# The block steps of the delta net's triangular inverse, eight heads at a time and on two quarters of the array

## The chip, the core and the metric

The kernel runs on one core of one Trainium2 chip. The metric is the time of one execution on the device in microseconds; the time of the kernel before is the median of 3 runs.

## What is computed

A block of two decoder layers and a third mixed layer on 256 tokens of width 1024, all in float32. The change lies in the first layer, a gated delta net with 16 value heads of width 128. The reference works in chunks of 64 tokens and solves a unit lower triangular system for each head and chunk:

```python
m = jnp.where(strict, jnp.einsum('bnhcd,bnhsd->bnhcs', k_beta, k) * decay, 0.0)
t_mat = lax.linalg.triangular_solve(m + eye, eye, left_side=True, lower=True, unit_diagonal=True)
u = jnp.einsum('bnhcs,bnhse->bnhce', t_mat, v_beta)
w = jnp.einsum('bnhcs,bnhsd->bnhcd', t_mat, k_beta * jnp.exp(gc)[..., None])
...
v_new = u_i - jnp.einsum('bhcd,bhde->bhce', w_i, state)
o_i = jnp.einsum('bhcd,bhde->bhce', qd_i, state) + jnp.einsum('bhcs,bhse->bhce', a_i, v_new)
```

The output of each head is normalized, gated with silu(z) and multiplied by `w_out`; convolution-gated feed-forward layers and two kinds of attention follow.

## The kernel before

The kernel computes the same with two blocks of 128 tokens (`tt` = 0, 1) per head instead of four chunks of 64. `XA` holds for each head three 128x128 blocks: the two diagonal ones (index 0 and 2) and the one across (index 1); `EA` holds the same of the decayed query-key products. The inverse of a diagonal block is made in levels. `inv_stage` inverts all 32x32 diagonal blocks by substitution on VectorE, with tokens of four blocks on the partitions, and DMAs write them back into `XA` and, transposed, into `T64`, which lies in the memory of `h`. Then come two doublings, 32 to 64 and 64 to 128: with inverses A and B of two neighbouring blocks and the block C between them, the new corner is a product of three, made in two steps. `y1` (line 823) and `z1` (lines 833, 834) are these steps for 32x32 blocks, `y2` (847) and `z2` (855) for 64x64. Each matmul of `y1` uses a 32x32 tile of the array, and `j` = 0, 2 are two tiles in different row and column groups; `z1` has a third. `y2` reads partitions 0 to 63 and writes 64 to 127 (the quarter of the rows `lo` and columns `hi`); `z2` reads 64 to 127 and writes 0 to 63. Between the steps ScalarE and VectorE copy the results out of PSUM (lines 824, 825, 835 to 838, 848, 857).

`chain(q4)` does this for four heads and then their recurrence: `y0p` (867), `x10p` (873), `y1p` (879), the outputs `o0p` and `o1p` (890 to 894), squares on ScalarE (898), a small chain of [128, 8] operations for the reciprocal root (905 to 910, with `rsqrt` at 334 to 338), eight scalings with silu(z) (913), and the transposes `otp` (921), whose copies `oh`, `ol` are the operands of the output product. `z` was parked in DRAM (`wzd`, line 803), and comes back by POOL's DMA as `wzog` (886) into a buffer that `kT` and `qT` hold before.

The order of the work: `gemm` and `gemm_nat` run the weight products in program order, and after every four weight tiles `w` calls `tick`, which advances each generator in `self.sides` by one `yield`. So the chains' pieces are strewn between the products of `w_in` (`pb`; 512 columns wide for z). `CY` = 2 and `CZ` = 2 ticks lie between a chain's steps. A chain starts when the chain before it has done its levels:

```python
def chain(q4):
    while not (st["inv"] and st["v"] >= 2 * q4 + 2 and st["lev"] >= q4):
        yield
```

Before `y0p` it also waits until `og` of the chain two before is counted. The products with `w_out` (`acc`) start when three of chain 0's heads are there. A list scheduler then sets each engine's order by its own estimate. Each weight block of 128x1024 is split by ScalarE into `wh` (line 186) and by VectorE into `wl` (187), and each product is three matmuls (249 to 251). PSUM has 8 banks; `acc` holds four. PE, ScalarE, VectorE and POOL each work in order.

Of the kernel before, what the change touches and what calls it, by code (L numbers as in the profile page):

```python
# [13 lines left out]
AF = mybir.ActivationFunctionType  # L14
# [5 lines left out]
P = 128  # L20
# [98 lines left out]
CY = 2  # L119
# [23 lines left out]
class Builder:  # L143
# [432 lines left out]
    def gdn_body(self, gp, x):  # L576
        nc, tc, sp = self.nc, self.tc, self.sp
        big = lambda nm: gp.tile([P, 8, T], F32, tag="big", bufs=2, name=nm)
        t4 = lambda sh, nm, dt=F32: gp.tile(sh, dt, tag="t4", bufs=2, name=nm)
        t2 = lambda sh, nm, dt=F32: gp.tile(sh, dt, tag="t2", bufs=6, name=nm)  # L580
        blk = lambda b: slice(32 * b, 32 * b + 32)
# [140 lines left out]
        def a_stage():  # L722
            while st["X"] < 8 or st["qss"] < 4 or st["step"] < AWAIT:
                yield
            factors(16)
            nc.vector.tensor_scalar(rq, rk.rearrange("p (a c) -> p a c", c=8)[:, 2:4], P ** -0.5, None, ALU.mult)
            for j in range(8):
                kq = self.bank("kq")
                nc.tensor.matmul(kq[:, 0:T], kT[:, j, 0:P], qT[:, j], start=True, stop=True)
                nc.tensor.matmul(kq[:, T:384], kT[:, j, P:], qT[:, j, P:], start=True, stop=True)  # L730
                for h in (2 * j, 2 * j + 1):
                    nc.vector.scalar_tensor_tensor(EA[:, h, 0:2], ev2(kq[:, 0:T]), negc[:, h : h + 1], EA[:, h, 0:2], ALU.mult, ALU.mult)
                    nc.vector.scalar_tensor_tensor(EA[:, h, 2], kq[:, T:384], negc[:, 16 + h : 17 + h], EA[:, h, 2], ALU.mult, ALU.mult)
                st["A"] = j + 1
                for _ in range(ASTEP):
                    yield
# [5 lines left out]
        T64 = self.h.rearrange("p a t -> p (a t)").rearrange("p (a h c) -> p a h c", a=2, h=16)  # L742
# [65 lines left out]
        hs = lambda i: slice(i * P, i * P + P)  # L808
        oks = {}

        def chain(q4):
            while not (st["inv"] and st["v"] >= 2 * q4 + 2 and st["lev"] >= q4):
                yield
            H = slice(4 * q4, 4 * q4 + 4)
            heads = range(4 * q4, 4 * q4 + 4)
            cs = slice(512 * q4, 512 * q4 + 512)
            Y1 = t2([P, 2, 4, 32], "Y1")
            b = self.bank("y1p")
            bv = b[:, 0:256].rearrange("p (a h c) -> p a h c", a=2, h=4)
            for tt in range(2):  # L820
                for i, h in enumerate(heads):
                    for j in (0, 2):
                        nc.tensor.matmul(bv[blk(j + 1), tt, i], XA[blk(j), h, 2 * tt, blk(j + 1)], T64[blk(j), tt, h, 0:32], start=True, stop=True)
            nc.scalar.activation(Y1[blk(1)], bv[blk(1)], AF.Copy)
            nc.vector.tensor_copy(Y1[blk(3)], bv[blk(3)])
            for _ in range(CY):
                yield
            b = self.bank("z1p")
            bv = b.rearrange("p (k a h c) -> p k a h c", k=2, a=2, h=4)
            for tt in range(2):  # L830
                for i, h in enumerate(heads):
                    for j in (0, 2):
                        nc.tensor.matmul(bv[blk(j), 0, tt, i], Y1[blk(j + 1), tt, i], XA[blk(j + 1), h, 2 * tt, blk(j + 1)], start=True, stop=True)
                    nc.tensor.matmul(bv[blk(1), 1, tt, i], XA[blk(1), h, 2 * tt, blk(1)], Y1[blk(1), tt, i], start=True, stop=True)
            nc.scalar.activation(T64[blk(1), :, H, 0:32], bv[blk(1), 1], AF.Copy)
            for tt in range(2):
                nc.vector.tensor_copy(XA[blk(0), H, 2 * tt, blk(1)], bv[blk(0), 0, tt])
                nc.scalar.activation(XA[blk(2), H, 2 * tt, blk(3)], bv[blk(2), 0, tt], AF.Copy)
            for _ in range(CY):
                yield  # L840
            lo, hi = slice(0, 64), slice(64, 128)
            Y2 = t2([P, 2, 4, 64], "Y2")
            b = self.bank("y2p")
            bv = b.rearrange("p (a h c) -> p a h c", a=2, h=4)
            for tt in range(2):
                for i, h in enumerate(heads):
                    nc.tensor.matmul(bv[hi, tt, i], XA[lo, h, 2 * tt, hi], T64[lo, tt, h], start=True, stop=True)  # L847
            nc.scalar.activation(Y2[hi], bv[hi], AF.Copy)
            for _ in range(CY):
                yield  # L850
            b = self.bank("z2p")
            bv = b.rearrange("p (a h c) -> p a h c", a=2, h=4)
            for tt in range(2):
                for i, h in enumerate(heads):
                    nc.tensor.matmul(bv[lo, tt, i], Y2[hi, tt, i], XA[hi, h, 2 * tt, hi], start=True, stop=True)  # L855
# [9 lines left out]
            b = self.bank("y0p")  # L865
# [5 lines left out]
            b = self.bank("x10p")  # L871
# [5 lines left out]
            b = self.bank("y1p")  # L877
# [1058 lines left out]
```

## Time and profile before

| | |
|---|---|
| median of 3 runs | 1217.02 us (1215.78 to 1218.51) |
| the profiled execution | 1216.23 us |
| its span | 1214.4 us |
| granted TensorE clock | 0.997 |
| PE, PEld busy | 98%, 93% of the span |
| DVE, ACT, POOL busy | 74%, 57%, 2% |

The span is the time from the first to the last instruction in the profile. PE is TensorE's matmuls, PEld its weight loads, DVE is VectorE, ACT is ScalarE, POOL is GpSimd. A line of a timeline gives the start, the length of the group from its first start to its last end, the operation with output <- inputs, and, in brackets, how long the engine had been idle and what released it. Matmuls are pipelined: their lengths overlap, and the distance between starts is what one takes of PE's time. In the names, `a<-b,c` leaves out buffer numbers; `xh`, `xl` are the split input.

### The profile page before, as it was taken

What the parts mean: (1) busy time and instruction counts of PE and PEld (TensorE: products, weight loads), DVE (VectorE), ACT (ScalarE), POOL (GpSimd) and SP (SyncE); (2) the same over time, 40 slices, a digit from 0 to 9 for tenths busy, and PEclk for the clock granted to TensorE, in tenths of its full rate; (3) what the DMA queues carried; (4) which work ended last, traced back from release to release, by engine and by line L of the source; (5) the groups of instructions that cost most, each with busy time, mean ns of one, the idle gap of its engine ahead of it and who ended that gap; (6) DMA issues with size and microseconds to landing.
All of it is one profiled execution on the core that took longest, in us unless ns stands there. A gap on an engine that the chain in (4) does not pass through costs nothing.

```text
span 1214.4 us, 23416 instructions
## 1 busy us (share of the span) xinstructions
PE 1188.7 (98%) x9368; PEld 1125.4 (93%) x9368; DVE 895.2 (74%) x1680; ACT 687.7 (57%) x1170; POOL 20.4 (2%) x47
## 2 busy tenths in 40 slices
PE   7999989999999999999999999999999999999997
PEld 6989878999999999889999999889789999999996
DVE  6978976668877778878977778756756567655555
ACT  5785547546655556656755556754465445444443
POOL 1000000000000000000000000000000000000000
PEclk9999999999999999999999999999999999999999
DMA  6546365355555557435555564364255563555552
GB/s 222 179 132 216 125 192 183 124 157 168 199 184 182 187 179 243 126 115 161 190 188 183 187 191 158 112 207 134 87 161 173 188 234 118 186 179 187 189 179 83
DMA packets 68318, 206.01 MB, mean 170 GB/s; under 512 B 18198, under 2 KB 18342, under 8 KB 67953
## 3 DMA queue, kind: packets, MB, share of 16 engines
q1 hardware_dynamic: 65600, 194.77, 50.3%
q0 software_dynamic: 2608, 9.75, 2.2%
q8 instruction: 73, 1.20, 0.4%
q14 instruction: 37, 0.29, 0.1%
HBM read 199.75 MB, written 4.74 MB: 168 GB/s over the span
## 4 chain that ended last, share of the span: by engine, by line
PE 92%; DVE 4%; ACT 2%; DMA 1%; issue 1%; SPq 0%; DVEq 0%; ACTq 0%
PE pb L249 21%; PE pb L250 20%; PE pb L251 20%; PE acc L249 7%; PE acc L250 7%; PE acc L251 7%; DVE wl L187 1%; PE pt L1138 1%; PE ssb L669 1%; DMA wr<-wall 0%; DMA h<-xT 0%; PE z2p L855 0%; PE y2p L847 0%; PE kv L1542 0%; PE csum L366 0%
## 5 line engine op out<-in xcount | busy, mean ns | idle before, releaser
L187 DVE TENSOR_TENSOR wl<-wr,wh 128x1024 fp32r<-128x1024 f32 x362 | 441.5, 1223 | 193.7 <-ACT wh L186 192.3
L186 ACT ACTIVATE wh<-wr 128x1024 fp32r<-128x1024 f32 x362 | 381.6, 1057 | 338.3 <-issue 101.1
L251 PE MATMUL pb<-xh,wl 128*128 128x256 f32 x1224 | 345.6, 283 | 3.9 <-DVE wl L187 3.9
L249 PE MATMUL pb<-xh,wh 128*128 128x256 f32 x1224 | 347.8, 284 | 0.6 <-ACT xh L569 0.6
L250 PE MATMUL pb<-xl,wh 128*128 128x256 f32 x1224 | 345.5, 282 | 0.2 <-DVE xl L570 0.2
L249 PEld LDWEIGHTS pb<-xh,wh 128*128 128x128 f32 x1224 | 231.7, 189 | 2.8 <-issue 1.3
L251 PEld LDWEIGHTS pb<-xh,wl 128*128 128x128 f32 x1224 | 229.7, 188 | 4.5 <-DVE wl L187 4.5
L250 PEld LDWEIGHTS pb<-xl,wh 128*128 128x128 f32 x1224 | 230.1, 188 | 0.5 <-DVE xl L570 0.4
L249 PE MATMUL pb<-fh,wh 128*128 128x256 f32 x416 | 118.3, 285 | 0.0
L250 PE MATMUL pb<-fl,wh 128*128 128x256 f32 x416 | 117.5, 283 | 0.1
L251 PE MATMUL pb<-fh,wl 128*128 128x256 f32 x416 | 116.6, 281 | 0.0
L249 PE MATMUL acc<-ah,wh 128*128 128x256 f32 x352 | 98.7, 280 | 0.0
L251 PE MATMUL acc<-ah,wl 128*128 128x256 f32 x352 | 98.5, 280 | 0.0
L250 PE MATMUL acc<-al,wh 128*128 128x256 f32 x352 | 98.5, 280 | 0.0
L249 PEld LDWEIGHTS pb<-fh,wh 128*128 128x128 f32 x416 | 77.9, 188 | 1.4 <-issue 0.4
L250 PEld LDWEIGHTS pb<-fl,wh 128*128 128x128 f32 x416 | 78.1, 188 | 1.1 <-DVE fl L436 0.3
L251 PEld LDWEIGHTS pb<-fh,wl 128*128 128x128 f32 x416 | 78.9, 190 | 0.0
L977 DVE SCALAR_TENSOR_TENSOR fy<-fpad,cols,fy 128x256 f32<-128x256 f32 x176 | 73.6, 478 | 0.0
L249 PE MATMUL pb<-wh,xh 128*128 128x512 f32 (+1 forms) x176 | 70.5, 402 | 0.0
L250 PE MATMUL pb<-wl,xh 128*128 128x512 f32 (+1 forms) x176 | 68.1, 387 | 0.5 <-DVE wl L187 0.5
L251 PE MATMUL pb<-wh,xl 128*128 128x512 f32 (+1 forms) x176 | 68.0, 387 | 0.0
L249 PEld LDWEIGHTS acc<-ah,wh 128*128 128x128 f32 x352 | 66.9, 190 | 0.0
(437 smaller groups left out, 2091.2 us busy)
## 6 DMA issues: line engine op xcount, KB each, us to landing
wr<-wall SPq DMA_DIRECT2D x362, 512.0 KB, 3.6
wzd<-zt POOLq DMA_DIRECT2D x8, 256.0 KB, 3.0
wzog<-wzd POOLq DMA_DIRECT2D x4, 512.0 KB, 5.2
bias<-bd POOLq DMA_DIRECT2D x4, 512.0 KB, 7.7
h<-xT SPq DMA_DIRECT2D x4, 256.0 KB, 4.0
h<-xT POOLq DMA_DIRECT2D x1, 1024.0 KB, 5.9
wrow<-wrow POOLq DMA_DIRECT2D x1, 1024.0 KB, 10.0
out_dram<-mw SPq DMA_DIRECT2D x4, 256.0 KB, 2.0
```

Of the source, the lines that this page charges most:

```text
L186: nc.scalar.activation(hi, r, AF.Copy)
L187: i = nc.vector.tensor_tensor(lo, r, hi.bitcast(F32), ALU.subtract)
L249: mm(out, ah, bh, start=start, stop=False, skip_group_check=skip)
L250: mm(out, ah, bl, start=False, stop=False, skip_group_check=skip)
L251: mm(out, al, bh, start=False, stop=stop, skip_group_check=skip)
L669: nc.tensor.matmul(ssb[:, c : c + 1], sq[:, i, tt * P : tt * P + P], self.ones[:, 0:1], start=True, stop=True)
L977: nc.vector.scalar_tensor_tensor(y[:, i], u[:, i, j : j + T], w(j), y[:, i], ALU.mult, ALU.add)
L1138: nc.tensor.transpose(pt[:, j * P : j * P + P], S[:, i, j * P : j * P + P], self.ident)
```

## The change

The levels leave `chain` and become one generator `levels` for all heads, with two batches of eight heads (`g` = 0, 1). A step's copies are 512 columns wide, `z1` has two banks (its third tile writes `z1q`), and `y2` and `z2` have a bank for each `tt`. The second batch is a step behind the first, and `yz2(1, 0)` issues `y2` of batch 1 and `z2` of batch 0 matmul by matmul in turns. `chain(q4)` starts when its batch has been counted in `lev`, so chains 0 and 1 start together, and chains 2 and 3.

```diff
+        def y1(g):
+            Y1[g] = t2([P, 2, 8, 32], "Y1")
+            b = self.bank("y1p")
+            for tt in range(2):
+                for i, h in enumerate(hds(g)):
+                    for j in (0, 2):
+                        nc.tensor.matmul(b4(b)[blk(j + 1), tt, i], XA[blk(j), h, 2 * tt, blk(j + 1)], T64[blk(j), tt, h, 0:32], start=True, stop=True)
+            nc.scalar.activation(Y1[g][blk(1)], b4(b)[blk(1)], AF.Copy)
+            nc.vector.tensor_copy(Y1[g][blk(3)], b4(b)[blk(3)])
+
+        def z1(g):
+            b0, b1 = self.bank("z1p"), self.bank("z1q")
+            for tt in range(2):
+                for i, h in enumerate(hds(g)):
+                    for j in (0, 2):
+                        nc.tensor.matmul(b4(b0)[blk(j), tt, i], Y1[g][blk(j + 1), tt, i], XA[blk(j + 1), h, 2 * tt, blk(j + 1)], start=True, stop=True)
+                    nc.tensor.matmul(b4(b1)[blk(1), tt, i], XA[blk(1), h, 2 * tt, blk(1)], Y1[g][blk(1), tt, i], start=True, stop=True)
...
+        def yz2(gy, gz):
...
+            for tt in range(2):
+                for i in range(8):
+                    if gy is not None:
+                        h = 8 * gy + i
+                        nc.tensor.matmul(b3(by[tt])[hi, i], XA[lo, h, 2 * tt, hi], T64[lo, tt, h], start=True, stop=True)
+                    if gz is not None:
+                        h = 8 * gz + i
+                        nc.tensor.matmul(b3(bz[tt])[lo, i], Y2[gz][hi, tt, i], XA[hi, h, 2 * tt, hi], start=True, stop=True)
...
+                st["lev"] += 2
+
+        def levels():
+            while not st["inv"]:
+                yield
+            steps = [lambda: y1(0), lambda: (z1(0), y1(1)), lambda: (yz2(0, None), z1(1)), lambda: yz2(1, 0), lambda: yz2(None, 1)]
+            for f in steps:
+                f()
+                for _ in range(CY):
+                    yield
+
         def chain(q4):
-            while not (st["inv"] and st["v"] >= 2 * q4 + 2 and st["lev"] >= q4):
+            while st["lev"] <= q4 or st["v"] < 2 * q4 + 2:
                 yield
...
-            for tt in range(2):
-                for i, h in enumerate(heads):
-                    nc.tensor.matmul(bv[hi, tt, i], XA[lo, h, 2 * tt, hi], T64[lo, tt, h], start=True, stop=True)
-            nc.scalar.activation(Y2[hi], bv[hi], AF.Copy)
-            for _ in range(CY):
-                yield
...
-            for tt in range(2):
-                nc.vector.tensor_copy(XA[lo, H, 2 * tt, hi], bv[lo, tt])
-            st["lev"] += 1
...
+        self.side(levels())
         for q4 in range(4):
             self.side(chain(q4))
```

How the instructions of the engines move shows in their order. First PE in the block steps, before. The listing names an fp32 matmul once; the trace shows two records of it. The `pb` rows are products of `w_in`.

```order
L823 MATMUL y1p<-h,XA 32x32 x15
L833 MATMUL z1p<-XA,Y_1976 32x32
...
L833 MATMUL z1p<-XA,Y_1976 32x32
L834 MATMUL z1p<-Y_1976,XA 32x32
L833 MATMUL z1p<-XA,Y_1976 32x32 x2
L834 MATMUL z1p<-Y_1976,XA 32x32
...
L847 MATMUL y2p<-h,XA 64x64 x8
...
L855 MATMUL z2p<-XA,Y_2105 64x64 x8
L823 MATMUL y1p<-h,XA 32x32 x16
```

And after:

```order
L825 MATMUL y1p<-h,XA 32x32 x31
L834 MATMUL z1p<-XA,Y_1976 32x32
L835 MATMUL z1q<-Y_1976,XA 32x32 x16
L825 MATMUL y1p<-h,XA 32x32 x19
L834 MATMUL z1p<-XA,Y_1976 32x32 x16
L825 MATMUL y1p<-h,XA 32x32 x13
...
L834 MATMUL z1p<-XA,Y_1976 32x32 x15
...
L849 MATMUL y2p<-h,XA 64x64 x8
L849 MATMUL y2q<-h,XA 64x64 x8
L834 MATMUL z1p<-XA,Y_2104 32x32 x2
L835 MATMUL z1q<-Y_2104,XA 32x32
...
L849 MATMUL y2p<-h,XA 64x64
L852 MATMUL z2p<-XA,Y_2200 64x64
```

The steps of four heads stood apart, between products; now those of eight heads stand together, the first `z1` with its third tile (`z1q`) on its own, the later one with three tiles in turn, and the middle pass with `y2` and `z2` in turn.

Second, VectorE at the same place, where `wl` is what the next products of `w_in` read and `EA` needs the product `kq` on PE. Before:

```order
L732 SCALAR_TENSOR_TENSOR EA<-kq,fac,EA 128x256
L733 SCALAR_TENSOR_TENSOR EA<-kq,fac,EA 128x128
L187 TENSOR_TENSOR wl_2002<-wr_1917,wh_2001 128x1024
L732 SCALAR_TENSOR_TENSOR EA<-kq,fac,EA 128x256
L187 TENSOR_TENSOR wl_2081<-wr_1949,wh_2080 128x1024
```

And after:

```order
L187 TENSOR_TENSOR wl_2018<-wr_1917,wh_2017 128x1024
...
L187 TENSOR_TENSOR wl_2158<-wr_1949,wh_2157 128x1024
...
L187 TENSOR_TENSOR wl_2264<-wr_2015,wh_2263 128x1024
L732 SCALAR_TENSOR_TENSOR EA<-kq,fac,EA 128x256
L733 SCALAR_TENSOR_TENSOR EA<-kq,fac,EA 128x128
```

The `wl` that stood behind a pair of `EA` operations now stand, three of them, ahead of it.

Third, the place where the products of `w_in` end and those of `w_out` begin. PE before:

```order
L249 MATMUL pb<-wh_2265,xh 128x512
L250 MATMUL pb<-wl_2266,xh 128x512
L251 MATMUL pb<-wh_2265,xl 128x512
L873 MATMUL x10p<-yy,XA 128x128 x4
L847 MATMUL y2p<-h,XA 64x64 x8
L921 MATMUL otp<-ident,wzog 128x128 x8
L879 MATMUL y1p<-r_2433,XA 128x128 x4
L890 MATMUL o0p<-yy,EA 128x128 x4
L855 MATMUL z2p<-XA,Y_2490 64x64 x8
L823 MATMUL y1p<-h,XA 32x32 x16
L249 MATMUL acc<-oh,wh_2307 128x256
```

PE after:

```order
L249 MATMUL pb<-wh_2427,xh 128x512
L250 MATMUL pb<-wl_2428,xh 128x512
L251 MATMUL pb<-wh_2427,xl 128x512
L937 MATMUL otp<-ident,wzog 128x128 x5
L883 MATMUL y0p<-vn,XA 128x128 x6
L937 MATMUL otp<-ident,wzog 128x128 x3
L883 MATMUL y0p<-vn,XA 128x128 x2
L937 MATMUL otp<-ident,wzog 128x128 x8
L249 MATMUL acc<-oh,wh_2516 128x256
...
L889 MATMUL x10p<-yy,XA 128x128 x8
```

and VectorE after, from the second chain's small operations on (`rq_2527` and `rq_2554` are the factors of chains 0 and 1):

```order
L921 TENSOR_TENSOR sc<-ms,rq_2554 128x8
L336 TENSOR_TENSOR rst<-rsy 128x8
L922 TENSOR_TENSOR sc<-sc,rq_2554 128x8
...
L926 SCALAR_TENSOR_TENSOR sc<-rsy,rq_2527 128x8
L336 TENSOR_TENSOR rst<-rsy 128x8
L929 SCALAR_TENSOR_TENSOR wzog<-o0p,sc,wzog 128x128 x4
L929 SCALAR_TENSOR_TENSOR wzog<-o1p,sc,wzog 128x128 x4
L337 SCALAR_TENSOR_TENSOR rst<-rst,sc 128x8
L187 TENSOR_TENSOR wl_2678<-wr_2514,wh_2677 128x1024
...
L926 SCALAR_TENSOR_TENSOR sc<-rsy,rq_2554 128x8
L929 SCALAR_TENSOR_TENSOR wzog<-o0p,sc,wzog 128x128 x4
L929 SCALAR_TENSOR_TENSOR wzog<-o1p,sc,wzog 128x128 x4
```

Before, the transposes of one chain stand there, with other steps of the next ones behind them; now those of two chains, with `y0p` of the next pair between, and ahead of all `acc`. VectorE does the small operations of two chains in turns, and a `wl` stands between their scalings.

## Rows read from the trace of the kernel before

**Rows 1.** The page: span, and busy time of PE and its weight loads.

```profile
span 1214.4 us, 23416 instructions
PE 1188.7 (98%) x9368; PEld 1125.4 (93%) x9368; DVE 895.2 (74%) x1680; ACT 687.7 (57%) x1170; POOL 20.4 (2%) x47
```

**Rows 2.** Busy time by stretch: start:end, length, PE, PEld, DVE, ACT, POOL, clock, DMA share, GB/s.

```profile
163.00:183.00 20.00, 17.81 (x241) 16.18 (x241) 13.57 (x29) 7.88 (x14) 0.00 (x0) 1.00 0.58 189
...
206.50:277.00 70.50, 70.34 (x698) 68.73 (x697) 45.91 (x116) 38.70 (x95) 2.70 (x5) 1.00 0.44 145
```

**Rows 3.** Timeline of PE, 163 to 200 us: start, length, count, [idle <- releaser].

```profile
169.75 0.24 PE L833 MATMUL z1p<-XA,Y 32*32 32x32 f32 x2 [0.46 <-ACT Y L824]
...
173.67 0.28 PE L249 MATMUL pb<-xh,wh 128*128 128x256 f32 x1
173.88 1.14 PE L847 MATMUL y2p<-h,XA 64*64 64x64 f32 x16
...
175.17 0.28 PE L251 MATMUL pb<-xh,wl 128*128 128x256 f32 x1
...
178.07 0.39 PE L251 MATMUL pb<-xh,wl 128*128 128x256 f32 x1 [1.72 <-DVE wl L187]
...
180.33 0.28 PE L251 MATMUL pb<-xh,wl 128*128 128x256 f32 x1
...
181.62 0.69 PE L823 MATMUL y1p<-h,XA 32*32 32x32 f32 x32
...
182.46 0.28 PE L250 MATMUL pb<-xl,wh 128*128 128x256 f32 x1
...
184.11 1.05 PE L867 MATMUL y0p<-vn,XA 128*128 128x128 f32 x8
185.09 0.22 PE L833 MATMUL z1p<-XA,Y 32*32 32x32 f32 x2
...
185.60 0.19 PE L834 MATMUL z1p<-Y,XA 32*32 32x32 f32 x1
...
186.06 0.40 PE L250 MATMUL pb<-wl,xh 128*128 128x512 f32 x1
...
186.99 0.40 PE L251 MATMUL pb<-wh,xl 128*128 128x512 f32 x1
```

**Rows 4.** Durations in ns, min/median/max, of the steps' matmuls and copies (views by tile).

```profile
L847 PE MATMUL y2p<-h,XA x64: 218/218/267, 173.9 to 223.7; 64*64 64x64 f32 x64
...
L824 ACT ACTIVATE Y<-y1p x4: 374/375/376, 169.3 to 213.1; 32x256 f32<-32x256 f32 x4
...
L848 ACT ACTIVATE Y<-y2p x4: 575/592/597, 177.3 to 225.6; 64x512 f32<-64x512 f32 x4
```

**Rows 5.** The z copies: POOL's timeline, issue to landing (page), and the silu behind them.

```profile
190.17 1.07 POOL L886 DMA_DIRECT2D wzog<-wzd  x2 [27.78 <-PE kq L730]
...
wzog<-wzd POOLq DMA_DIRECT2D x4, 512.0 KB, 5.2
...
L887 ACT ACTIVATE wzog<-wzog x4: 1048/1057/1059, 195.2 to 233.1; 128x1024 f32<-128x1024 f32 x4
```

**Rows 6.** Timelines of PE, ScalarE and VectorE at the end of chain 3.

```profile
248.31 0.37 PE L249 MATMUL acc<-oh,wh 128*128 128x256 f32 x1
...
254.05 0.33 PE L921 MATMUL otp<-ident,wzog 128*128 128x128 f32 x1
...
248.59 0.28 ACT L898 ACTIVATE wzog<-o1p 128x128 f32<-128x128 f32 x1 [0.54 <-PE o1p L894]
...
249.77 0.17 DVE L905 TENSOR_TENSOR sc<-ms,rq 128x8 f32<-128x8 f32 x1 [0.46 <-ACT wzog L898]
...
253.64 1.13 DVE L913 SCALAR_TENSOR_TENSOR wzog<-o0p,sc,wzog 128x128 f32<-128x128 f32 x4
```

**Rows 7.** The page's costliest groups: VectorE's `wl`, busy us and mean ns.

```profile
L187 DVE TENSOR_TENSOR wl<-wr,wh 128x1024 fp32r<-128x1024 f32 x362 | 441.5, 1223 | 193.7 <-ACT wh L186 192.3
```

**Rows 8.** Waits of PE's weight loads, 163 to 277 us: total, times, longest.

```profile
PEld otp L921 <- DVE wzog L913: 0.5, 2, 0.3
```

More of the change, by code (lines that the diff above doesn't have):

```diff
@@ L809, in gdn_body @@
         oks = {}
+        lo, hi = slice(0, 64), slice(64, 128)
+        Y1, Y2 = {}, {}
+        hds = lambda g: range(8 * g, 8 * g + 8)
+        h8 = lambda g: slice(8 * g, 8 * g + 8)
+        b4 = lambda b: b.rearrange("p (a h c) -> p a h c", a=2, h=8)
+        b3 = lambda b: b.rearrange("p (h c) -> p h c", h=8)
+        def y1(g):
[7 more added lines that the diff above has]
+            nc.vector.tensor_copy(Y1[g][blk(3)], b4(b)[blk(3)])
@@ new lines, in z1 @@
+        def z1(g):
[5 more added lines that the diff above has]
+                    nc.tensor.matmul(b4(b1)[blk(1), tt, i], XA[blk(1), h, 2 * tt, blk(1)], Y1[g][blk(1), tt, i], start=True, stop=True)
+            H = h8(g)
+            nc.scalar.activation(T64[blk(1), :, H, 0:32], b4(b1)[blk(1)], AF.Copy)
+            for tt in range(2):
+                nc.vector.tensor_copy(XA[blk(0), H, 2 * tt, blk(1)], b4(b0)[blk(0), tt])
+                nc.scalar.activation(XA[blk(2), H, 2 * tt, blk(3)], b4(b0)[blk(2), tt], AF.Copy)
@@ new lines, in yz2 @@
+        def yz2(gy, gz):
+            by = [self.bank("y2p"), self.bank("y2q")] if gy is not None else None
+            bz = [self.bank("z2p"), self.bank("z2q")] if gz is not None else None
+            for tt in range(2):
+                for i in range(8):
[5 more added lines that the diff above has]
+                        nc.tensor.matmul(b3(bz[tt])[lo, i], Y2[gz][hi, tt, i], XA[hi, h, 2 * tt, hi], start=True, stop=True)
+            if gy is not None:
+                Y2[gy] = t4([P, 2, 8, 64], "Y2")
+                for tt in range(2):
+                    nc.scalar.activation(Y2[gy][hi, tt], b3(by[tt])[hi], AF.Copy)
+            if gz is not None:
+                for tt in range(2):
+                    nc.vector.tensor_copy(XA[lo, h8(gz), 2 * tt, hi], b3(bz[tt])[lo])
+                st["lev"] += 2
@@ L816, in chain @@
             cs = slice(512 * q4, 512 * q4 + 512)
-            Y1 = t2([P, 2, 4, 32], "Y1")
-            b = self.bank("y1p")
-            bv = b[:, 0:256].rearrange("p (a h c) -> p a h c", a=2, h=4)
-            for tt in range(2):
-                for i, h in enumerate(heads):
-                    for j in (0, 2):
-                        nc.tensor.matmul(bv[blk(j + 1), tt, i], XA[blk(j), h, 2 * tt, blk(j + 1)], T64[blk(j), tt, h, 0:32], start=True, stop=True)
-            nc.scalar.activation(Y1[blk(1)], bv[blk(1)], AF.Copy)
@@ L825, in chain @@
-            nc.vector.tensor_copy(Y1[blk(3)], bv[blk(3)])
-            for _ in range(CY):
-                yield
-            b = self.bank("z1p")
-            bv = b.rearrange("p (k a h c) -> p k a h c", k=2, a=2, h=4)
-            for tt in range(2):
[L831 to L844, printed above, removed]
@@ L845, in chain @@
-            for tt in range(2):
-                for i, h in enumerate(heads):
-                    nc.tensor.matmul(bv[hi, tt, i], XA[lo, h, 2 * tt, hi], T64[lo, tt, h], start=True, stop=True)
-            nc.scalar.activation(Y2[hi], bv[hi], AF.Copy)
[L849 to L855, printed above, removed]
@@ L856, in chain @@
-            for tt in range(2):
-                nc.vector.tensor_copy(XA[lo, H, 2 * tt, hi], bv[lo, tt])
-            st["lev"] += 1
-            for _ in range(CY):
-                yield
             while st["og"] < q4 - 1:
```

## The prediction

> **What bounds the kernel now.** I read the page first: TensorE (PE) is busy for 98% of the span [rows 1], so the end moves by PE work that goes or comes and by PE's waits, and by little else. Then the busy time by stretch, to find the stage of the change: it lies between 163 and 277 us, where the granted clock is full throughout; in the first 20 us PE is idle for 2.2, in the last 70 for 0.2 [rows 2]. So behind 183 us no latency of the chains is open: other heads' steps and the weight products cover it. Two idle times of the stage have names: 0.46 us for ScalarE's first Y copy and 1.72 us for a `wl` of VectorE [rows 3]. PE's timeline then prices the steps.
>
> **Prices of the steps.** An order row of one fp32 matmul is two records in the trace. Sixteen records of a 64x64 step span 1.14 us [rows 3] and one lasts 0.22 [rows 4]: a record every 0.058 us. The 32 records of `y1p`, in turns on two tiles, span 0.69 us with 0.19 for one: every 0.016. The 48 of `z1p`, in turns on three, start from 185.09 to 185.60: every 0.011. A 128-wide record comes every 0.111 (eight of `y0p` and a change of tile size in 0.98) [rows 3], some twice as long as a 64-wide one; so a 32-wide one alone should take about 0.031, and two tiles give half of that and three a third. **Tiles in different row groups overlap fully**, and I take that for two 64x64 quarters too. Beside the records a visit to small tiles costs a constant: the `y2p` visit takes 1.50 us from a weight product ahead to the second behind it, less two ordinary spacings of 0.12 is 1.26, less 16 x 0.058 leaves 0.33; a visit with two sizes (`z2p`, then `y1p`) takes 2.13 - 0.24 - 0.92 - 0.50 = 0.47 [rows 3].
>
> **The block steps before.** `y1` 128 records x 0.016 = 2.0; `z1` 192 x 0.011 = 2.1; `y2` and `z2` 128 x 0.058 = 7.4: 11.5 us. By its order chain 0 makes six visits (one head of `y1`, the rest with the start of `z1`, two pieces of `z1`, `y2`, and `z2` with chain 1's `y1`), chains 1 and 2 three each (`z1`, `y2`, `z2` with the next `y1`), chain 3 three: fifteen, three of them with two sizes, 12 x 0.33 + 3 x 0.47 = 5.4. With the two waits of 2.2 that is 19.1 us on PE's path.
>
> **After.** `y1` stays 2.0. The first `z1` breaks up: its third tile has a bank of its own and runs alone (16 matmuls, 32 records x 0.031 = 1.0), the other two 64 x 0.016 = 1.0; the second keeps three tiles in turn, 96 x 0.011 = 1.05. Of the 64x64 steps the first and the last pass run alone, 32 x 0.058 = 1.84 each; the middle one has 64 records on two quarters, 1.84 with full overlap, 3.68 without: 5.5. That is 10.6 us. Visits fall from fifteen to six: 5 x 0.33 + 0.47 = 2.1. The wait for the first Y copy grows, since the copy is twice as wide and nothing stands between: a 256-wide one takes 0.375, a 512-wide one 0.592 [rows 4], so 0.46 + 0.22 = 0.68. The 1.72 us wait goes: it came of two `EA` products on VectorE ahead of `wl`, which waited for `kq`; in the order after, three `wl` stand ahead of them, and PE arrives later. Together 13.4 us, **5.7 less**. For a lone 32-wide tile the bounds are 0.016 and 0.058 (0.5 to 1.9 us for the 32 records); 0.031 is between, by the column count. The copies are half as many and twice as wide, on engines that are not full [rows 2]: nothing on PE's path beyond the one wait.
>
> In the middle pass the rows, two tiles at 0.016 and three at 0.011, speak for full overlap [rows 3]. The Trainium skill ("TensorE: Matmul & The Clock Gate", section "Measured speedup vs the span model") gives 2.38 times for three tiles at once; by that ratio of 0.79 the pass would take an estimated 2.3 us, and the gain would be 0.5 us smaller. The step from two tiles to three in this trace, 1.44 of a possible 1.5, agrees better with full overlap.
>
> **What is moved: heads run in pairs of chains.** Chains 0 and 1 now start together once `lev` is 2, then 2 and 3. The w_in products, which cover latency, are no more than before, and by the order after they are used up just when the normalization of both chains is due. Count from the end of the last `kq`, K. PE has 32 records of `y1p`/`o0p` (3.6), six 512-wide products (0.233 each, 1.4), 32 records of `o1p` (3.6), twelve products (2.8), `vtp` (0.4), twelve products (2.8): the first `otp` is due at K + 14.5. POOL issues the two z copies (`wzog`) only when `kq` is done, as before, some 0.3 behind it and 0.5 apart, and they land 5.2 us later [rows 5]: K + 5.6 and 6.1. ScalarE, in its order, waits for them and then does silu (1.06 [rows 5]), three squares (1.2 for four [rows 6], say 0.75), silu, a square, a `wh` (1.06), then the eight squares of `o1p`: K + 11.8. VectorE's small operations run from 249.77 to 253.64 for one chain, with one `wl` of 1.2 among them: 2.7 [rows 6, 7]; two chains in turns, I say 2.0 behind the last square. Four scalings take 1.13 with 0.34 for one, so 0.26 each [rows 6]; `otp` needs the sixth for its first four: K + 15.4, against 14.6 for PE, a wait of 0.8. Behind it VectorE ends chain 0 at K + 15.9, does a `wl` (1.2), five small ones (1.0) and chain 1's eight scalings (2.1): K + 20.2, where PE, with 0.8 lost, eight `y0p` (1.8) and sixteen `otp` (1.4) done, could have been at 18.5: 1.7 us of wait less the little that overlaps, with the `acc` products queued behind the `otp` on PE. I take **2.5 in all**. For the second pair `acc` products are there as cover: 46 of them and eight `otp` stand between `o1p` and `otp` of chain 3, 46 x 0.12 + 0.7 = 6.2 us (48 took 5.74 before [rows 6]); squares 1.2, small ones 2.7, one `wl` 1.2 and six scalings 1.6 come to 6.7: a wait of 0.5 or so, as much as PE's loads wait at that place before [rows 8]. So the moved chains give back 2.5 + 0.5 less the 0.5 that was there, some 2.5 to 2.7; I take 2.7, between 0 (z copies and ScalarE early) and 7.7 (rival 3). `xT` is read back into `h` earlier on POOL, ahead of the z copies, while the DMA engines are about half busy [rows 2]; `h` is last read by the second `y2`, before the last `kq`, so it holds up nothing there. SyncE's order of issues is the same row by row.
>
> **Sum.** -5.7 + 2.7 = -3.0 us. The profiled execution took 1216.2, 1.8 of it around the span, and lies 0.8 below the median of the runs; from the median 1217.0 the forecast is **1214.0**. About 0.2%, 2.4 us, is what a measurement can tell from no change.
>
> **Rivals.** (1) *The chains' waits don't appear*: if the z copies or ScalarE's queue are 2 us sooner, the first pair is covered and the whole 5.7 stays: 1211.3. For it: PE is idle for 0.2 of 70 us in this stage before. Against: there a chain's latency had another chain's steps as cover; now both stand at one point. (2) *The quarters don't overlap*, the change doesn't do what it says: 1.84 more, 1215.8. For it: no row shows 64x64 tiles in turns. Against: the rows of 32x32 ones. (3) *Slower: the ends of the chains, done one behind the other, become the bound.* If VectorE's two small chains and sixteen scalings of a pair run serially with two `wl` between (K + 11.8 + 5.4 + 4.2 + 2.4 = K + 23.8 against 18.5), the first pair waits 5.3 us, and the second, with another `wl` ahead (1.2) and all its eight scalings and an `ol` behind, some 2.9: 8.2, less the 0.5 that was there, so 7.7 against 5.7. It decides from 5.7 us of waits on: 1219.0. Against: the order after has the first pair's small operations in turns.
>
> **How the numbers follow.** Forecast 0.50, rival 1 0.25, rival 2 0.12, rival 3 0.13. The forecast's own spread, 1212.5 to 1215.7 by the waits, lies for 0.6 of it under 1214.6, which with rival 1 makes faster by over 0.2%: 0.30 + 0.25 = 0.55. Slower by over 0.2% (above 1219.5) needs rival 3 with still longer waits: 0.05. Between: 0.40. The range goes from 1210.5 (rival 1 with half a us to spare) to 1217.5, and leaves out most of rival 3 and the tail of rival 1.
>
> **What would show it.** Right: the middle pass has a record every 0.029 us; six visits; the 1.72 us wait of `wl` is gone; 0.7 us of wait ahead of the first `z1p`; PE waits 2 to 3 us for `wzog` scalings at `otp` right behind the last w_in product; the out product ends some 3 us earlier than 277. Wrong: a record every 0.058 in the middle pass; no wait at `otp`; a new wait for `wl` or for the `z2` copies ahead of `y0p`; the stretch behind 277 us longer or shorter by itself.

## The result, and the profile after

The changed kernel takes **1225.14 us** (median of 4, 1224.99 to 1229.86) against 1216.84 for the kernel before on the same chip: a ratio of 1.0077 [1.0055, 1.0100], 8.3 us slower, where 3.0 us faster was forecast. The profiled execution is the longest of the four (1229.86 us), and its mean granted clock the lowest (0.989; 0.991, 0.992 and 0.992 in the others), so it shows more of the low clock than the median has. The page of after; before stands in [rows 1]:

```profile
span 1228.0 us, 23405 instructions
PE 1197.2 (97%) x9368; PEld 1133.2 (92%) x9368; DVE 893.0 (73%) x1670; ACT 685.3 (56%) x1162; POOL 20.2 (2%) x47
```

PE is busy for 8.5 us *more*, though it has fewer and denser visits to make. The busy time by stretch (columns as in [rows 2]; the granted clock is the third number from the end) says why:

```profile
163.00:183.00 20.00, 18.69 (x310) 17.51 (x309) 8.68 (x19) 4.68 (x9) 0.79 (x2) 0.76 0.49 155
173.40:190.60 17.20, 16.57 (x265) 15.68 (x262) 7.55 (x14) 8.83 (x15) 0.00 (x0) 0.51 0.13 37
206.50:277.00 70.50, 63.32 (x493) 59.92 (x492) 39.31 (x116) 35.93 (x99) 3.10 (x6) 0.98 0.41 142
224.50:227.80 3.30, 3.30 (x16) 3.30 (x17) 2.29 (x8) 0.60 (x1) 0.00 (x0) 0.50 0.35 139
```

Before, the clock was 1.00 in the first and third of these stretches. Now it is 0.50 (1.2 GHz instead of 2.4) from about 173.3 to 190.3 us and from 224.5 to 227.9. PE's timeline at the places of the change:

```profile
170.00 1.19 PE L825 MATMUL y1p<-h,XA 32*32 32x32 f32 x62
171.87 0.21 PE L834 MATMUL z1p<-XA,Y 32*32 32x32 f32 x1 [0.68 <-ACT Y L826]
...
171.93 1.05 PE L835 MATMUL z1q<-Y,XA 32*32 32x32 f32 x28
...
174.48 0.69 PE L834 MATMUL z1p<-XA,Y 32*32 32x32 f32 x18 [0.63 <-issue]
...
176.19 0.41 PE L250 MATMUL pb<-xl,wh 128*128 128x256 f32 x1
176.41 0.41 PE L251 MATMUL pb<-xh,wl 128*128 128x256 f32 x1
```

Here one reads, in order: `y1` of eight heads; the wait for the Y copy, 0.68 us as forecast; the third tile's lone run, 28 records from 171.93 to 172.79, 0.031 each, as forecast; then a second idle time that was not, 0.63 us "issue": no other engine is named. It starts at 173.85, when the clock has been low for 0.6 us. The last two rows show the low clock: two 256-wide products start 0.22 us apart, where at 1.00 it is 0.12. Later on the same timeline:

```profile
192.37 0.27 PE L849 MATMUL y2p<-h,XA 64*64 64x64 f32 x1
...
194.23 0.22 PE L852 MATMUL z2q<-XA,Y 64*64 64x64 f32 x1
194.38 0.39 PE L249 MATMUL pb<-xh,wh 128*128 128x256 f32 x1
```

This is the middle pass, at full clock again: 64 records from 192.37 to 194.23, **0.029 us each: the two quarters overlap in full**. (The ratio of 2.38 for three tiles, from the Trainium skill, "TensorE: Matmul & The Clock Gate", section "Measured speedup vs the span model", would have made it an estimated 2.3 us; the measurement decides.) And PE's waits from 163 to 300 us: total, times, longest.

```profile
PE otp L937 <- DVE wzog L929: 3.5, 3, 2.7
PE acc L249 <- ACT oh L435: 2.6, 2, 1.7
...
PE acc L250 <- DVE ol L436: 0.6, 1, 0.6
PE o1p L909 <- DVE wzog L929: 0.5, 1, 0.5
```

Before, PE itself had only the 0.5 us at `z1p` and the 1.7 us for `wl` in this stage [rows 3]; the 0.5 us of [rows 8] is that of its weight loads. The longest of the waits after is on the timelines of PE and, behind it, VectorE:

```profile
221.13 0.59 PE L937 MATMUL otp<-ident,wzog 128*128 128x128 f32 x3 [0.37 <-DVE wzog L929]
224.38 0.43 PE L937 MATMUL otp<-ident,wzog 128*128 128x128 f32 x1 [2.66 <-DVE wzog L929]
224.60 2.77 PE L883 MATMUL y0p<-vn,XA 128*128 128x128 f32 x12
```

```profile
219.69 1.13 DVE L929 SCALAR_TENSOR_TENSOR wzog<-o0p,sc,wzog 128x128 f32<-128x128 f32 x4
220.73 1.11 DVE L929 SCALAR_TENSOR_TENSOR wzog<-o1p,sc,wzog 128x128 f32<-128x128 f32 x4
...
221.84 1.22 DVE L187 TENSOR_TENSOR wl<-wr,wh 128x1024 fp32r<-128x1024 f32 x1
...
223.97 1.13 DVE L929 SCALAR_TENSOR_TENSOR wzog<-o0p,sc,wzog 128x128 f32<-128x128 f32 x4
```

VectorE scales chain 0 until 221.84, does a `wl`, ends the small operations of chain 1 and begins its scalings at 223.97; the fifth `otp` on PE waits for that 2.66 us, and twelve records of `y0p`, which need nothing from it, stand behind it in PE's queue.

So there are three suspects: the pairs' waits, the low clock, and the stop without a releaser. The expectations of the first four runs set two theories against each other: that closely packed small-tile work brings the clock down (T), and that the waits do the harm, in themselves and by the clock (W).

### The profile page after: what moved, and what is told of

It reads as the page before. It is cut to its first block, busy times and chain, and to the rows that moved or that the text cites. A ratio compares the mean times of both kernels' runs of the same rounds, so it can differ in the third digit from the quotient of the medians.

```text
span 1228.0 us, 23405 instructions
## 1 busy us (share of the span) xinstructions
PE 1197.2 (97%) x9368; PEld 1133.2 (92%) x9368; DVE 893.0 (73%) x1670; ACT 685.3 (56%) x1162; POOL 20.2 (2%) x47
## 4 chain that ended last, share of the span: by engine, by line
PE 74%; DVE 2%; ACT 1%; issue 0%; DVEq 0%; ACTq 0%
PE pb L249 17%; PE pb L250 17%; PE pb L251 17%; PE acc L249 6%; PE acc L250 6%; PE acc L251 6%; PE pt L1155 1%; PE kv L1559 0%; PE gob L1576 0%; ACT S L1122 0%; DVE wl L187 0%; PE ms L1472 0%; PE ob L1148 0%; PE mo L1506 0%; PE cs L485 0%
## 5 line engine op out<-in xcount | busy, mean ns | idle before, releaser
L250 PEld LDWEIGHTS pb<-xl,wh 128*128 128x128 f32 x1224 | 232.7, 190 | 0.3 <-DVE xl L570 0.2
```

The costliest lines, as they stand in the source:

```text
L250: mm(out, ah, bl, start=False, stop=False, skip_group_check=skip)
```

## Experiments

**Passes apart, chains apart.** `e_spread` gives each pass a step of its own; `e_stagger` holds a chain back until the one before has its squares; `e_both` does both. `e_dense` is the kernel *before* with chain 1's `y1` issued seven times (the result stays the same).

```diff
-steps = [lambda: y1(0), lambda: (z1(0), y1(1)), lambda: (yz2(0, None), z1(1)), lambda: yz2(1, 0), lambda: yz2(None, 1)]
+steps = [lambda: y1(0), lambda: z1(0), lambda: y1(1), lambda: yz2(0, None), lambda: z1(1), lambda: yz2(1, 0), lambda: yz2(None, 1)]   # e_spread
...
-            while st["lev"] <= q4 or st["v"] < 2 * q4 + 2:
+            while st["lev"] <= q4 or st["v"] < 2 * q4 + 2 or st["ch"] < q4:   # e_stagger
...
+            st["ch"] += 1
...
-                    for j in (0, 2):
+                    for j in (0, 2) * (7 if q4 == 1 else 1):   # e_dense
```

- `e_spread`. 

> The changed kernel with one edit: its five steps become seven, so that the first z1 and the second y1, and the first y2 and the second z1, no longer share a step, and weight products stand between. The pairs of chains stay. Theory (clock): small-tile matmuls in a row, 170.0 to 177 and 181.9 to 187.3 us of the changed kernel's profile, leave the array so little in use that TensorE's granted clock falls to 0.5 for 17 us (173.4 to 190.7), and half of that, 8.6 us, is the loss. It expects the clock to stay at 1.00 from 163 to 215 us and the time to fall from 1225.1 by 6 to 9 us, to 1216 to 1219; the waits at otp stay at 2 to 4 us, with a short fall of the clock behind them. Rival (waits): the paired chains' waits at otp and the idle times are the loss, and the clock hardly matters. It expects 1223 or more, since all those waits stay.


- `e_stagger`. 

> The changed kernel with one edit: a chain begins y0p only when the chain before it has issued its o1p squares, so chains run one behind the other and not in pairs; the block steps stay as changed. Theory (clock): the stretch at clock 0.5 around 173 to 191 us stays, with its loss of about 7 to 9 us; the otp waits (3.5 us) and the second fall of the clock (224.5 to 227.9 us) go, so some 4 to 5 us: 1220 to 1221. Rival (waits): without the waits the whole forecast gain of 5.7 us is there: 1211 to 1214.


- `e_both`. 

> Both edits together: seven steps, and chains one behind the other. Theory (clock) and rival (waits) both expect it below the kernel before: clock 1.00 from 163 to 277 us, no otp wait over 1 us, and the block steps 4 to 5.7 us cheaper (eight visits to small tiles and one wait for the Y copy): 1211 to 1214. If it stays above 1217, both are incomplete and something else in the block steps costs time.


- `e_dense`. 

> The kernel before with one edit: chain 1's y1 matmuls are issued seven times in a row instead of once, each writing the same result, 192 more records of 32x32 in turns on two tiles, with no wait added. Their own time is 192 x 0.016 = 3.0 us. Theory (clock): 224 such records in a row behind the z2 step make 4.7 us of small tiles without a pause, so the granted clock falls to 0.5 for several us though PE does not wait: 1217 + 3 + 2 to 6 = 1222 to 1226. Rival (the clock falls only where PE stands idle): clock 1.00, and 1220 from the records alone.

Against 1217.21 for the kernel before: `e_spread` **1233.88** (1.0136 [1.0121, 1.0152]), `e_stagger` **1217.48** (1.0003 [0.9989, 1.0016]), `e_both` **1223.22** (1.0047 [1.0027, 1.0067]), `e_dense` **1220.66** (1.0028 [1.0018, 1.0038]). `e_stagger` fell between the two theories, and neither had put `e_spread` at 1234 or `e_both` above the kernel before. What keeps `e_both` there are new waits (2.5 us at `x10p`, 2.5 at `otp`) and the clock, low for 6.8, 3.4 and 3.4 us in its profile. Its ten executions go with their mean granted clock: 1217.20 us at 0.997, 1231.74 at 0.984. The windows of `e_spread`, with the low clock first behind the lone `z1q`, then behind the pair's `otp`:

```profile
172.20:178.40 6.20, 6.20 (x81) 5.62 (x80) 2.99 (x8) 2.15 (x4) 0.00 (x0) 0.52 0.02 7
220.00:231.00 11.00, 7.03 (x34) 6.48 (x35) 6.92 (x29) 2.57 (x4) 0.17 (x1) 0.53 0.00 1
```

In the second PE is busy for 7.0 of 11 us: `otp` waits 7.3 us in all, as I read it because spread passes use up the w_in products sooner. Staggered chains lose this wait and the low clock behind it; the first fall stays, from 175.9 to 182.7 us in `e_stagger`. PE's waits in `e_stagger`, 163 to 300 us:

```profile
PE z1p L834 <- issue: 1.2, 1, 1.2
PE z1p L834 <- ACT Y L826: 0.7, 1, 0.7
PE otp L938 <- DVE wzog L930: 0.4, 1, 0.4
```

`e_dense` is T's test, and T fell: 224 records in pairs, one behind the other, and the clock stays up.

```profile
181.73 3.73 PE L823 MATMUL y1p<-h,XA 32*32 32x32 f32 x224
```

```profile
181.80:185.40 3.60, 3.60 (x226) 3.56 (x225) 1.05 (x3) 0.00 (x0) 0.00 (x0) 1.00 0.88 313
185.00:190.00 5.00, 4.81 (x98) 4.14 (x92) 3.30 (x6) 3.04 (x6) 0.00 (x0) 1.00 0.36 123
```

**The wait, the lone tile.** `e_yy` fills the Y wait with `y1` of batch 1; `e_triple` puts the third tile into the free rows of the same bank, so that the scheduler keeps the three in turn; `e_lone` is the kernel before with extra records on one tile; `e_yy_trip_stag` joins the first two with `e_stagger`.

```diff
+steps = [lambda: (y1(0), y1(1)), lambda: z1(0), lambda: (yz2(0, None), z1(1)), lambda: yz2(1, 0), lambda: yz2(None, 1)]   # e_yy
...
-            b0, b1 = self.bank("z1p"), self.bank("z1q")
+            b0 = self.bank("z1p")   # e_triple, and b0 for b1 below
...
+                    for j in (0, 2) + ((0,) * 6 if q4 == 1 else ()):   # e_lone
```

- `e_yy`. 

> The changed kernel with y1 of batch 1 moved ahead of z1 of batch 0, so that its 64 records stand where PE waited 0.68 us for the first Y copy. The lone run of z1q (32 records on one 32x32 tile, 1.0 us) stays. Theory I (the granted clock falls behind an idle stop of PE amid small-tile work): clock 1.00 from 163 to 220 us, the fall at the otp wait (2.7 us) stays; 1217 to 1220. Rival L (it falls behind work on a lone tile): 0.50 from some 1 to 2 us behind z1q on as before, 1224 to 1225. Rival S (idle time and lone-tile time add up): no first fall, 1217 to 1220.


- `e_triple`. 

> The changed kernel with z1's third tile in the bank of the other two (rows 32 to 63, which they leave free), so that it runs in turn with them and the lone run of 1.0 us is gone; the wait for the first Y copy (0.68 us) stays. Theory I: the clock falls to 0.50 behind that wait, 1223 to 1226. Rival L: no first fall, 1217 to 1220. Rival S: no first fall either, or a later one; 1217 to 1222.


- `e_lone`. 

> The kernel before, in which chain 1's y1 issues six more matmuls per head and block on one and the same 32x32 tile (96 more records, results unchanged), with no idle time of PE. At 0.037 us for a lone record that is 3.5 us. Theory I: the clock stays 1.00, 1217.2 + 3.5 = 1220.7. Rival L, and S: it falls to 0.50 for 8 us or more, 1224 to 1226.


- `e_yy_trip_stag`. 

> All three together: y1 of batch 1 ahead of z1 of batch 0, z1's tiles in turn, and each chain held back until the one before has its squares. Every theory of the clock: 1.00 throughout 163 to 290 us. The waits at otp are 0.4 us in all, those of acc for oh and ol gone. 1225.1 less 6.7 of clock less 4 to 6 of waits: 1212 to 1214, below the kernel before (1217). If the order of the chains costs what it saves: 1217.

Against 1216.91: `e_yy` **1226.07** (1.0076 [1.0058, 1.0093]), `e_triple` **1224.34** (1.0064 [1.0039, 1.0089]), `e_lone` **1222.58** (1.0043 [1.0026, 1.0060]), `e_yy_trip_stag` **1211.71** (0.9963 [0.9951, 0.9976]). PE's timeline in `e_lone`, and its windows:

```profile
182.00 4.80 PE L823 MATMUL y1p<-h,XA 32*32 32x32 f32 x128
```

```profile
182.00:184.00 2.00, 2.00 (x75) 2.00 (x74) 1.11 (x3) 0.00 (x0) 0.00 (x0) 1.00 0.76 291
184.00:190.00 6.00, 6.00 (x70) 5.45 (x67) 1.75 (x3) 1.90 (x3) 0.00 (x0) 0.50 0.40 153
```

No idle time, seven of eight records on one tile, and the clock falls: theory I fell as the only cause. In `e_triple` no tile runs alone, yet it falls at 171.6 us, at the end of the second of two dense passes with the 0.68 us wait between them, ahead of the stop of 1.0 us that this kernel has too (172.7 to 173.7): L fell as the only cause too.

```profile
169.00:171.60 2.60, 1.92 (x120) 1.81 (x112) 1.51 (x4) 0.59 (x1) 0.00 (x0) 1.00 0.80 321
171.60:188.00 16.40, 15.40 (x263) 14.24 (x257) 7.39 (x13) 8.59 (x14) 0.00 (x0) 0.50 0.21 63
```

What is left is S: stretches in which PE stands still and stretches on one small tile count together. In `e_yy`, where I expected the clock to stay, another idle time had come in:

```profile
169.06 2.21 PE L825 MATMUL y1p<-h,XA 32*32 32x32 f32 x124
171.43 0.21 PE L834 MATMUL z1p<-XA,Y 32*32 32x32 f32 x1 [0.17 <-ACT Y L826]
173.37 1.11 PE L835 MATMUL z1q<-Y,XA 32*32 32x32 f32 x17 [1.27 <-issue]
```

The Y wait is down to 0.17 us, but PE stops for 1.27 in the midst of `z1q`. The stop doesn't explain the fall, though: the clock goes down at 172.12 us, 0.02 behind its beginning. Ahead of the fall stand 2.2 us in pairs, the short wait and the lone run. In the changed kernel, `e_stagger`, `e_yy`, `e_triple` and `e_yy_trip_stag` such a stop stands ahead of the same record, to within one. Two of them, counted from the start of the span to a moment within the stop (PE's busy time and, in brackets, its records):

```profile
0.00:174.30 174.30, 162.68 (x1237) 149.09 (x1237) 141.04 (x329) 105.53 (x185) 8.34 (x21) 1.00 0.56 181
```

```profile
0.00:173.00 173.00, 160.59 (x1237) 147.39 (x1237) 142.28 (x331) 106.27 (x186) 8.53 (x21) 1.00 0.58 182
```

1237 records in both, though one is a `z1p` and the other a `z1q`.

**The stop's place.** 44 records more at the start of the kernel, in the 6.1 us in which PE waits for VectorE: `e_shift` is the changed kernel with these, `e_all_shift` has the three edits of `e_yy_trip_stag` too, and `e_sp1_all` and `e_all_seq` change one thing more in `e_all_shift`.

```diff
             warm(WARM[0], self.ones)
+            warm(22, self.ones[:, 0:1])
...
+steps = [lambda: (y1(0), y1(1)), lambda: z1(0), lambda: yz2(0, None), lambda: z1(1), lambda: yz2(1, 0), lambda: yz2(None, 1)]   # e_sp1_all
...
+lambda: (yz2(1, None), yz2(None, 0)),   # e_all_seq, for yz2(1, 0)
```

- `e_shift`. 

> The changed kernel with 22 more one-column matmuls (44 records) on PE at the start, where it waits 6.1 us for VectorE; their results are not read. Theory C: the stop without a releaser (0.6 to 1.3 us) that five of the kernels have at PE's record 1237, whatever operation that is, some 4.2 to 4.9 us behind record 1109, is the arrival of PE's next instructions. With 44 more records ahead, records 1109 and 1237 lie in other work, over 5.5 us apart: no stop, 1225.1 less 0.6 to 1.2 = 1224 to 1224.5, and 1220 to 1222 if the clock then stays up longer. Rival: the stop belongs to z1 (a wait that the profile does not show): it stays at the same matmul of z1, 1225.


- `e_all_shift`. 

> The three edits of the fastest kernel so far (1211.7) and the 44 records ahead. Theory C: no stop of 1.0 us in z1, and with it no low clock behind it (3 us at 0.50, 1.5 us): 1209 to 1210.5. Rival, the stop belongs to z1: 1211.7.


- `e_sp1_all`. 

> The same, with y2 of batch 0 and z1 of batch 1 as steps of their own, so that products of w_in stand between all passes but y1's. If passes of small tiles close together still cost clock: 1.00 throughout and 1209 to 1210.5, 1 us or so less than with them together. If the clock is full there already: 0.3 us more for a visit, no difference that can be measured.


- `e_all_seq`. 

> The same as the second kernel of this call, but with y2 of batch 1 and z2 of batch 0 one behind the other, not in turn on the two quarters. If the quarters overlap in full, as the 64 records in 1.86 us of the changed kernel say, this takes 1.84 us more. If a third of it is hidden anyway, 1.2. If 3.7 us on one 64x64 quarter at a time bring the clock down: 4 us or more, with 0.50 behind the pass.

Against 1218.33: `e_shift` **1226.07** (1.0063 [1.0046, 1.0080]), `e_all_shift` **1214.34** (0.9964 [0.9951, 0.9976]), `e_sp1_all` **1217.76** (0.9996 [0.9987, 1.0004]), `e_all_seq` **1214.14** (0.9960 [0.9947, 0.9972]). The stop is gone in all four, so it belongs to a place in PE's instruction stream and not to an operation. It was not there either in `e_spread` and `e_both`, where weight products stand around this record. But the 44 records cost 0.21 us each and outlasted the gap, so that all that follows starts 3 us later. In `e_shift` the clock still falls, for 6.8 us in the block steps. PE's timeline in `e_all_shift`, and the clock through the whole stage:

```profile
0.99 11.68 PE L554 MATMUL warm<-ones 128*128 128x128 f32 x54 [0.99 <-POOL ones L524]
12.53 0.99 PE L366 MATMUL csum<-ones,sqa 128*128 128x1 f32 x4
```

```profile
163.00:277.00 114.00, 111.95 (x1245) 106.98 (x1245) 76.76 (x178) 65.42 (x147) 6.03 (x14) 1.00 0.52 168
```

`e_sp1_all` was a miss: no clock to win there, and passes spread out make the chains late (`o1p` waits 1.5 us for `yy`, `y1p` 0.8). `e_all_seq` was a surprise: with the quarters one behind the other the pass is 1.7 us longer, and the time the same.

All profiles together say more than S did. The Y wait of 0.68 us, the lone `z1q` and the stop are three separate troubles of the block steps. Each of the nine kernels with the steps of eight heads that has one or more of them has the low clock there, for 3.4 to 17.1 us; each of the six that have none (`e_all_shift`, `e_sp1_all`, `e_all_seq`, and below `e_pairs`, `e_all_fill`, `e_seq_fill`) keeps 1.00. The wait without a lone run is `e_triple`, the lone run with 0.17 us of wait `e_yy`, the stop with neither `e_yy_trip_stag`; these are single profiles.

**The shares.** Four kernels with 44 records of 32x32 at the start, which take 2.55 us there and end well inside the gap: `e_fill` is the changed kernel with these alone, `e_pairs` adds the edits of `e_yy` and `e_triple`, `e_all_fill` those and `e_stagger`, `e_seq_fill` also the quarters one behind the other. (The fourth kernel of the list in the text on `e_pairs`, and the staggered one, is `e_all_fill`.)

```diff
+            for _ in range(22):
+                nc.tensor.matmul(wb[0:32, 0:32], self.ones[0:32, 0:32], self.ones[0:32, 0:32], start=True, stop=True)
```

- `e_fill`. 

> The changed kernel with 22 small matmuls (44 records of 32x32, results not read) at the start, where PE waits 6.1 us; the 44 one-column records on the full array took 0.21 us each and moved the start of everything by 3 us. At 0.06 each these end before that wait does, so they cost nothing. By theory C the stop in z1 (0.6 to 1.2 us) is gone and nothing else: 1224 to 1224.5. If the clock then falls later and for less time, as with the one-column records (7.6 us at half clock for 17.3): 1220 to 1222.


- `e_pairs`. 

> The chains in pairs, as in the changed kernel, but with the other three causes away: y1 of batch 1 ahead of z1 of batch 0, z1's tiles in turn, and the 44 small records at the start. This prices the pairing. By the waits of the changed kernel (7.2 us at otp, o1p and acc) and the low clock behind the longest (3.4 us, 1.7 lost), against 0.4 us in the staggered kernel: 7 to 8.5 us over the fourth kernel of this call's list, 1217 to 1219. If most of the waits come only of the late start of the chains: 1212 to 1214.


- `e_all_fill`. 

> The same as the kernel with the three edits that took 1211.7, and the 44 small records: no stop, clock 1.00 throughout, 1.0 + 1.5 less: 1209 to 1210.5. If the z copies or vt set the end of the stage anyway: 1211 to 1212.


- `e_seq_fill`. 

> The same as the kernel before it in this call, with the middle y2 and z2 one behind the other. Before, with the one-column records, this took as long as with the quarters in turn (1214.1 against 1214.3), though the pass itself was 1.7 us longer: there vtp waited 0.7 us less. If the gain of the quarters is given back at vtp: 0 to 1 us more. If that was chance: 1.7 us more.

Against 1217.48: `e_fill` **1224.68** (1.0059 [1.0042, 1.0076]), `e_pairs` **1222.05** (1.0036 [1.0024, 1.0048]), `e_all_fill` **1212.35** (0.9964 [0.9949, 0.9980]), `e_seq_fill` **1214.05** (0.9970 [0.9959, 0.9981]). `e_fill` shows that in the changed kernel the stop alone is worth little: 7.2 us over its kernel before, where the change is 8.3 over its own, and the clock still falls twice (6.8 and 3.4 us). `e_pairs` is the one to read: clock and stop are cured in the block steps, and only the pairing is left.

```profile
PE otp L939 <- DVE wzog L931: 3.0, 2, 2.5
PE acc L249 <- ACT oh L435: 2.6, 2, 1.7
PE acc L250 <- DVE ol L436: 0.6, 1, 0.6
```

```profile
163.00:215.00 52.00, 49.79 (x716) 45.30 (x714) 33.41 (x88) 30.55 (x75) 3.67 (x7) 1.00 0.54 176
215.00:219.00 4.00, 3.45 (x17) 3.46 (x18) 2.92 (x10) 0.66 (x2) 0.00 (x0) 0.58 0.58 189
```

Its 6.0 us of waits more than in `e_all_fill` (0.6 in all) and some 1.7 us for the low clock behind the 2.5 us at `otp` are 7.7 of the 9.7 us between the two medians. From the first `y1` record to the first `acc<-ah` product the profiles differ by 8.9 us (146.7 against 137.8), so some 1.0 of the rest is work in this stage, and 0.8 lies outside it; what it is stays open. The quarters in turn are worth 1.7 us here (1214.05 - 1212.35), about the length of the pass that they save, and nothing in `e_all_shift` against `e_all_seq`, where `vtp` waited 1.5 us in the one and 0.8 in the other ahead of the block steps. The same stretch of the profiles, without that wait, says 1.1 us here (138.9 against 137.8) and 1.0 there (138.8 against 137.8). `e_all_fill` is no faster than `e_yy_trip_stag` against its own kernel before (5.1 and 5.2 us), so the medians don't show what the stop and the 3.4 us of low clock behind it cost; the profiles do: 140.1 us for that stretch in `e_yy_trip_stag` against 137.8, with 1.0 us of idle time and, at half of 3.4, an estimated 1.7 for the clock. Both are **faster than the kernel before by about 0.37%**, and by 13 us than the change.

## Why the prediction was wrong

One stretch holds the whole change, from the first `y1` record to the first `acc<-ah` product; before, after and in `e_all_fill` it is (columns as in [rows 2]):

```profile
164.35:308.00 143.65, 141.31 (x1455) 134.48 (x1455) 99.70 (x237) 82.96 (x178) 5.53 (x13) 1.00 0.48 159
165.75:321.42 155.67, 147.16 (x1455) 140.07 (x1454) 97.54 (x227) 80.57 (x170) 5.53 (x13) 0.93 0.43 146
164.98:302.78 137.80, 137.23 (x1454) 131.97 (x1454) 98.82 (x227) 80.46 (x170) 5.53 (x13) 1.00 0.50 166
```

After, it is 12.0 us longer than before. PE is idle for 8.5 us in place of 2.3: 6.2 more. The two low stretches, 17.1 and 3.4 us, cost an estimated half of their length, 10.2. Without them PE's busy time is 136.9 against 141.3: 4.4 less. That this remainder is work is borne out by `e_all_fill`, where the clock is full and PE busy for 137.2 us. These are the profiled executions; the median of the changed kernel lies 4.7 us below its profiled one, so there the clock costs less.

- *Block steps, "5.7 less".* Right for the work. It was forecast to fall by 4.2 us (16.9 to 12.7, the waits left out), and 4.4 is what the rows above show. `e_all_fill` is 5.1 us below the kernel before (by the interval 2.4 to 6.2), and this stretch 5.9 shorter in its profile; having lost the lone tile and most of the Y wait as well, it should have gained about 6.7 by the same prices. The parts were right too: the Y wait 0.68, the lone tile at 0.031 a record, the middle pass at 0.029. Rival 2 is out.
- *"The granted clock is full throughout".* This is the first step that failed. It was read from the kernel before and carried over without a term of its own. The change put together eight heads of 32-wide work, a wait with nothing to cover it, a lone tile and the stop at record 1237, and the clock fell to 0.50 there and again behind the long wait at `otp`: an estimated 10.2 us in the profiled execution. By medians the troubles of the block steps cost 3.7 us (the changed kernel is 8.3 us over the kernel before, `e_pairs`, which has lost them, 4.6). The sum had 0.22 for the longer wait and 0.5 for the lone tile, and nothing for clock or stop.
- *Pairs of chains, "I take 2.7".* The second failed step: right mechanism, wrong size. The waits at `otp`, `acc` and `o1p` are 7.2 us (3.5, 3.2 and 0.5), where 3.0 were forecast, and with the low clock behind them and some work that stays open the pairing costs 9.7 by medians. The timetable itself held. POOL's z copies, ScalarE's silu and its last square against K + 0.3, K + 5.6 and K + 11.8 (K is 206.1):

```profile
206.37 1.06 POOL L902 DMA_DIRECT2D wzog<-wzd  x2 [10.82 <-PE kq L730]
```

```profile
211.72 1.06 ACT L903 ACTIVATE wzog<-wzog 128x1024 f32<-128x1024 f32 x1 [2.21 <-DMA wzog<-wzd]
...
217.32 0.35 ACT L914 ACTIVATE wzog<-o1p 128x128 f32<-128x128 f32 x1
```

  They start at K + 0.3 and K + 5.6, and the last square ends at K + 11.6; chain 0's scalings end at K + 15.7 (15.9 forecast), and chain 1's at K + 20.0 (20.2). Three things were missed behind it. I let PE do `y0p` during the second wait, but in its order they stand behind the waiting `otp` (2.66 us, not 1.7). The wait brought the clock down for what followed. And for the second pair I counted up to `otp` (0.45 us there, as forecast) and not one step on, to the copies of `otp`:

```profile
272.63 0.74 PE L249 MATMUL acc<-oh,wh 128*128 128x256 f32 x4 [1.66 <-ACT oh L435]
...
273.98 0.38 PE L250 MATMUL acc<-ol,wh 128*128 128x256 f32 x1 [0.61 <-DVE ol L436]
```

  The `acc` products wait there for `oh` and `ol`, and 0.93 us for the first pair's `oh`: 3.2 us in all, for which the sum had nothing.
- *Rivals.* Rival 3 named the right side, and its 7.7 us of waits are nearer to the 7.2 measured than the forecast's 3.0. But that was luck: it had the two chains' small operations one behind the other and their scalings done at K + 23.8, and VectorE did them in turns, by K + 20.0, as the forecast had it; half of the waits stood at `acc` and `o1p`. With its waits alone the time would have been 1219.
- *Sum.* By medians, each against its own kernel before, the shares are -5.1 (`e_all_fill`), +9.7 (`e_pairs` over it) and +3.7 (the change over `e_pairs`). They add up to the measured 8.3 us because each is a step to the next kernel, which proves nothing by itself, and each has an uncertainty of some 2 us. The rows above price the causes without other kernels: +6.2 of waits and an estimated +10.2 of clock in the profiled execution, and the -4.4 that remain are close to the 4.2 forecast and to the 4.1 of `e_all_fill`.

## What to carry to other kernels

Making small passes denser saves what the trace prices, but price also what they were strewn between: the products between the steps hid the copies. That such products also hold the clock up was not shown: `e_spread` put them back between the passes, and with the Y wait and the lone tile still there the clock fell. When several chains become one batch, let their ends follow each other (one counter and one condition in the start of a chain turned 8 us of loss into none), and follow each chain to the first product that uses its result, not to its last own step. And when an engine waits, read in its order what stands behind the waiting instruction: work that is ready there is late as well.

## What the runs showed of the hardware

- TensorE's clock fell to half during 4.8 us on mostly one 32x32 tile without any idle time (`e_lone`), behind two dense passes with 0.68 us of waiting among them (`e_triple`), and behind waits of 2.1 to 3.3 us at `otp` and 1.6 us at `x10p` (`e_both`). It did not fall behind 3.7 us of 32x32 tiles in pairs (`e_dense`), behind 3.7 us on one 64x64 quarter at a time (`e_all_seq`), or behind the 1.72 us wait of the kernel before among full-width products [rows 3].
- In the low stretches 256-wide products start 0.22 us apart instead of 0.12, and each stretch lasted 3.4 to 17.1 us before the clock came back. Its length differs between executions of one kernel: the mean granted clock of `e_triple` went from 0.987 (1229.44 us) to 0.994 (1221.99).
- A run of small matmuls can stop PE for 0.6 to 1.3 us at a fixed record of its stream (1237 here) with no releaser shown; 44 records more ahead of it, and there is no stop. That PE's next instructions are late there fits this, and no run shows it directly.
- Two matmuls on different 64x64 quarters start together, 0.058 us for both; a one-column fp32 record on the full array still took 0.21 us at the start of the kernel, one on a 32x32 tile 0.058.
